# The RWKV recurrence step on ScalarE, and the mixers' steps planned by new durations behind the in-projection matmuls

## The chip, the cores and the metric

One core of a Trainium2 chip runs the whole program. It has five engines that each take their own instructions in order: TensorE (PE, matmuls; its weight loads are PEld), VectorE (DVE), ScalarE (ACT), GpSimd (POOL) and SyncE (SP), which issues the DMA transfers. The metric is the device time of one execution in microseconds (us), lower is better; the median of several runs is compared.

## The reference

One layer on 1024 tokens of width 1024: RMSNorm, a projection of every token to the inputs of three kinds of heads, the three mixers side by side, an output projection, a SwiGLU feed-forward, and a final norm, all in float32.

```python
h = rmsnorm(x, g1);  p = h @ w_in            # P_COLS columns, split in three
y = concat(mlstm_group(p_m), retention_group(p_r), rwkv7_group(p_w))
x = x + y @ w_out
x = x + swiglu(rmsnorm(x, g2));  out = rmsnorm(x, g3)
# RWKV-7, per frame t and head, state S (64 x 64):
S = S * w_t - (S kk_t) (kk_t * a_t)^T + v_t k_t^T;   y_t = S r_t
```

The RWKV recurrence is the one long serial dependence: six heads (three pairs), 1024 frames. The kernel takes it in chunks of 64 frames: inside a chunk a unit triangular 64 x 64 matrix is inverted, and from chunk to chunk a state of 64 x 64 per head is carried.

## The kernel before

**Phases.** The span has three parts. Until some 746 us the in-projection runs and the mixers run between its matmuls; then a rest of the output projection until some 811 us; then the feed-forward until the end. Only the first part is touched by the change. Every float32 product of a projection is made of three matmuls with operands split in a high and a low part: `split_hi` on ACT (L90, `whi`), `split_lo` on DVE (L93, `wlo`), matmuls L119 to L121 (512 columns) and L729 to L731 (256 columns), which all write a tile named `acc`. These are called dense matmuls here.

**What sets the order.** `weave` (L131) is a planner that runs in Python when the program is built. Each stream is a generator; a stream gives up its turn with `yield cost, latency`: its cost advances a planned clock, and it is due again after the latency. Streams `rwkv_chain`, `rwkv_inverse`, `rwkv_prep`, `rwkv_out`, `norms` and `attention` have precedence in this order; the in-projection's streams (`sharing`) fill what is left. `signal` and a yielded name let one stream wait for another. The instructions come out in the order in which the planner reached them, a scheduler then sets each engine's own order from that, and each engine keeps to it: an instruction whose wait isn't over holds up what stands behind it. The planner's numbers are `PART`, `LAT`, `CHAIN`, `INV`, `ATT`, `NORM`, `MIX` and the literals in the yields.

**The RWKV streams.** Per pair of heads and half of the sequence `rwkv_prep` makes, for 8 chunks, the matrices E (by DVE from the gram matmuls L460; transposes L480) and X. `rwkv_inverse` fetches the triangular blocks back from DRAM as MN, with one DMA (L507, 512 KB, each value on several partitions), has ACT copy a part of it to R (four copies, L509), and then solves on DVE in a row of dependent steps (L514 to L522); the result goes to DRAM (r_d) and comes back into E by four DMAs (L532); two transposes on DVE (L535) and matmuls L540 end it. `rwkv_chain` does the 48 steps of the recurrence (3 pairs x 16 chunks), each of five pieces of TensorE with a hand-over between: L581 (state against kappa), ACT copies the result to `pm` (L583); L586 with pm gives u, ACT copies u into X (L592, L593); L597 and L600 give the state's increment and the output; DVE makes the next state from old state, decay and increment and writes it straight into the next step's X (L607, two halves), POOL copies it to `st` (L609, two halves), and ACT copies the output to `yw` (L610) and squares it (L611). The next step's L581 reads that X.

**The other mixers.** `attention` runs the mLSTM and the retention by chunks of 128 tokens: `mlstm_load` fetches q, k, v and the gate weights `w`; it adds the causal mask (POOL L860) and takes exponentials (ACT L863), and `mlstm_chunk` uses them. `mlstm_gates` sends a few numbers by DMA through DRAM and scans them on DVE (L798). `rot` is the rotary table, one load of 512 KB at the start.

## Time and profile before

| | us |
|---|---|
| median of 3 runs (range) | 1515.08 (1514.54 to 1521.72) |
| the profiled execution | 1521.67 |
| its span, first to last instruction | 1519.9 |
| PE busy in it | 1425.6 (94%) |
| DVE, ACT, POOL busy | 892.4 (59%), 556.2 (37%), 437.9 (29%) |

The profiled execution is one of the runs; the trace's numbers add up to its span, 1519.9 us, with 1.8 us around it. Busy shares are means over three phases with different limits, so the reader has to look at the stretch that the change touches, at what the idle time of TensorE there ended with, and at the clock that was granted to TensorE: it has two levels, 2.4 GHz (shown as 1.0) and 1.2 GHz (shown as 0.5).

### The profile page before, as it was taken

The numbers are of one execution on the slowest core, as the hardware profiler recorded it, in microseconds if no ns is written. First come the engines' busy times: TensorE is split into PE (matmuls) and PEld (weight loads), VectorE is DVE, ScalarE is ACT, GpSimd is POOL, SyncE is SP. The second block draws the span as 40 slices with busy tenths as digits, with TensorE's granted clock in tenths as the row PEclk, the third lists the DMA queues.
The fourth block names the chain that finished last, engine by engine and source line by source line (L and its number), as shares of the span: only waits on it lengthen the run. The fifth ranks groups of instructions, "written<-read, shape, count | busy, mean of one in ns | idle before, by whom it ended". The sixth has DMA issues, their size and how long they took to land.

```text
span 1519.9 us, 23085 instructions
## 1 busy us (share of the span) xinstructions
PE 1425.6 (94%) x8434; PEld 1161.3 (76%) x8434; DVE 892.4 (59%) x1762; ACT 556.2 (37%) x1202; POOL 437.9 (29%) x539
## 2 busy tenths in 40 slices
PE   7998799789998998999998999999999998999996
PEld 5777577777777887887777887888888886887886
DVE  6457567458847756645468555555555565347434
ACT  6353334333432133244456333333333344224222
POOL 3211013234424333333545433344444420000000
PEclk9999999999978889899999999999999999999998
DMA  5142122334422244354632222222222247337333
GB/s 209 43 136 66 50 80 74 83 89 112 122 59 68 85 129 124 106 161 142 220 112 85 96 83 83 72 73 78 83 84 83 83 168 255 93 95 238 98 97 111
DMA packets 122269, 164.55 MB, mean 108 GB/s; under 512 B 38028, under 2 KB 70956, under 8 KB 120876
## 3 DMA queue, kind: packets, MB, share of 16 engines
q1 hardware_dynamic: 122156, 163.08, 33.5%
q8 instruction: 66, 1.08, 0.3%
q14 instruction: 47, 0.39, 0.1%
HBM read 124.75 MB, written 38.29 MB: 107 GB/s over the span
## 4 chain that ended last, share of the span: by engine, by line
PE 53%; DVE 3%; POOL 2%; DMA 2%; issue 1%; ACT 0%; POOLq 0%; DVEq 0%; SPq 0%; ACTq 0%
PE acc L1171 5%; PE acc L1172 5%; PE acc L1173 5%; PE chain L1365 5%; PE chain L1364 5%; PE chain L1366 5%; PE misc L1172 4%; PE misc L1171 4%; PE misc L1173 4%; PE acc L119 2%; PE acc L121 2%; PE acc L120 2%; DVE act L93 1%; PE acc L729 1%; PE acc L731 1%
## 5 line engine op out<-in xcount | busy, mean ns | idle before, releaser
L93 DVE TENSOR_TENSOR wlo<-wraw,whi 128x512 fp32r<-128x512 f32 (+1 forms) x210 | 147.9, 707 | 138.3 <-ACT whi L90 137.1
L90 ACT ACTIVATE whi<-wraw 128x512 fp32r<-128x512 f32 (+1 forms) x210 | 128.1, 612 | 226.3 <-PE chain L1365 117.9
L729 PE MATMUL acc<-whi,act 128*128 128x256 f32 (+1 forms) x512 | 161.3, 318 | 4.4 <-ACT whi L90 3.4
L90 ACT ACTIVATE whi<-rg 128x512 fp32r<-128x512 f32 x128 | 79.8, 631 | 228.7 <-POOL rg L1232 90.0
L730 PE MATMUL acc<-wlo,act 128*128 128x256 f32 (+1 forms) x512 | 155.4, 305 | 5.2 <-DVE wlo L93 5.2
L119 PE MATMUL acc<-act,whi 128*128 128x512 f32 x352 | 152.3, 433 | 7.0 <-ACT whi L90 6.2
L93 DVE TENSOR_TENSOR wlo<-rg,whi 128x512 fp32r<-128x512 f32 x128 | 93.1, 728 | 108.1 <-ACT whi L90 105.9
L731 PE MATMUL acc<-whi,act 128*128 128x256 f32 (+1 forms) x512 | 153.0, 300 | 0.0
L1364 PE MATMUL chain<-act,whi 128*128 128x512 f32 (+1 forms) x374 | 144.3, 386 | 4.0 <-ACT act L90 4.0
L120 PE MATMUL acc<-act,whi 128*128 128x512 f32 x352 | 145.5, 413 | 1.5 <-DVE act L252 1.5
L121 PE MATMUL acc<-act,wlo 128*128 128x512 f32 x352 | 145.7, 414 | 1.1 <-DVE wlo L93 1.1
L1365 PE MATMUL chain<-act,whi 128*128 128x512 f32 (+1 forms) x374 | 144.0, 385 | 0.5 <-DVE act L93 0.5
L1366 PE MATMUL chain<-act,wlo 128*128 128x512 f32 (+1 forms) x374 | 143.8, 384 | 0.0
L1171 PE MATMUL acc<-act,whi 128*128 128x512 f32 x352 | 139.3, 396 | 3.4 <-ACT pre L1432 2.7
L1173 PE MATMUL acc<-act,wlo 128*128 128x512 f32 x352 | 138.8, 394 | 0.0
L1172 PE MATMUL acc<-act,whi 128*128 128x512 f32 x352 | 138.5, 394 | 0.0
L729 PEld LDWEIGHTS acc<-whi,act 128*128 128x128 f32 x512 | 104.3, 205 | 12.1 <-ACT whi L90 3.9
L730 PEld LDWEIGHTS acc<-wlo,act 128*128 128x128 f32 x512 | 105.0, 206 | 9.2 <-DVE wlo L93 6.7
L731 PEld LDWEIGHTS acc<-whi,act 128*128 128x128 f32 x512 | 105.2, 206 | 1.0
L1172 PE MATMUL misc<-act,whi 128*128 128x512 f32 x264 | 104.1, 394 | 0.0
L1171 PE MATMUL misc<-act,whi 128*128 128x512 f32 x264 | 104.0, 394 | 0.0
L1173 PE MATMUL misc<-act,wlo 128*128 128x512 f32 x264 | 103.8, 393 | 0.0
(327 smaller groups left out, 2835.9 us busy)
## 6 DMA issues: line engine op xcount, KB each, us to landing
wraw<-in_w_down SPq DMA_DIRECT2D x85, 256.0 KB, 2.7
rg<-in_w_gate SPq DMA_DIRECT2D x22, 512.0 KB, 4.9
rg<-in_w_up SPq DMA_DIRECT2D x22, 512.0 KB, 5.0
a_dram<-work SPq DMA_DIRECT2D x41, 256.0 KB, 2.2
wraw<-in_w_tm SPq DMA_DIRECT2D x40, 256.0 KB, 3.0
rg<-a_dram SPq DMA_DIRECT2D x10, 1024.0 KB, 6.1
v_dram<-vt SPq DMA_DIRECT2D x64, 128.0 KB, 1.9
wraw<-in_w_out SPq DMA_DIRECT2D x32, 256.0 KB, 3.2
```

Source lines behind the costliest of these rows:

```text
L90: S.activation(hi, src, AF.Copy, scale=scale)
L93: (eng or V).tensor_tensor(lo, src, hi.bitcast(F32), ALU.subtract)
L119: PE.matmul(ps, lhsT=hi, rhs=xh[:, k, :], start=(k == 0), stop=False)
L729: PE.matmul(o, lhsT=xh[h][:, k, sl], rhs=w[k][0], start=(k == 0), stop=False)
L730: PE.matmul(o, lhsT=xh[h][:, k, sl], rhs=w[k][1], start=False, stop=False)
L731: PE.matmul(o, lhsT=xl[h][:, k, sl], rhs=w[k][0], start=False, stop=(k == KT - 1))
L1171: PE.matmul(ps, lhsT=hi, rhs=hi_x[:, k, :], start=(start and k == 0), stop=False, skip_group_check=True)
L1172: PE.matmul(ps, lhsT=hi, rhs=lo_x[:, k, :], start=False, stop=False, skip_group_check=True)
L1173: PE.matmul(ps, lhsT=lo, rhs=hi_x[:, k, :], start=False, stop=(stop and k == 3), skip_group_check=True)
L1364: PE.matmul(ps, lhsT=hi, rhs=hi_a[:, sl], start=(f == 0), stop=False)
L1365: PE.matmul(ps, lhsT=hi, rhs=lo_a[:, sl], start=False, stop=False)
L1366: PE.matmul(ps, lhsT=lo, rhs=hi_a[:, sl], start=False, stop=(f == FT - 1))
```

## The change

1. **Order.** Each step of a stream that is not the in-projection's is now issued inside `tc.issue_after(dense[0])`: its matmuls stay behind the last in-projection matmul that the planner had reached. `late(engine)` does the same against the last instruction of one engine, for the inverse's first DVE step, its transposes, the mask of the mLSTM weights, one product in `rwkv_out` and one split in `norms`. Nearly all costs and latencies of the planner are new.
2. **The chain.** E's layout is changed so that increment and output come from one pair of matmuls with 128 columns of weights (L627). ACT copies the increment alone into the next step's X (L633, two halves). What the decayed old state adds is made by POOL (`sd`, one product) and two more matmuls into the next step's tile (L619). DVE makes the next `st` beside that (L636, two halves), from the same PSUM tile; the POOL copies are gone. The output copy and its square are now two halves each (L640, L641). TensorE has 10 matmuls in a step before and after.
3. **The inverse.** R comes by a DMA of its own, 128 KB in pieces of 128 B, instead of the four ACT copies.
4. **The rest.** The mLSTM weights' mask and exponentials are made after the chunk before (`mlstm_weights`) instead of with the loads. `rot` comes in 24 loads of 64 KB, one per token tile and group, instead of one load. The gram matmuls keep their order.

```diff
-    clock, events = [0.0], {}
+            dense[0] = PE.matmul(ps, lhsT=lo, rhs=xh[:, k, :], start=False, stop=(k == KT - 1)).ins
+
+
+
+
+
+    clock, events = [10.0], {}
...
+            with nullcontext() if s[2] in sharing or dense[0] is None else tc.issue_after(dense[0]):
+                got = next(s[2], None)
             if s is holder:
...
-    PART = 6 * 0.214
+    PART, TOK = 6 * 0.23, 12 * 0.47e-3
...
     NT = 9
-    LAT = 0.93
-    CHAIN, INV, ATT, NORM, MIX = 3.51, 20.16, 3.09, 3.26, 1.28
...
-        yield 0.9, 5.5
+            V.tensor_tensor(E[rows, :, kap(q)], c3(kk)[rows], er[rows, :, 0:64], ALU.mult)
+            G.tensor_tensor(E[rows, :, rcp(q)], c3(r)[rows], er[rows, :, 1:65], ALU.mult)
+        yield 1.2, 7.0
...
+            prev = None
+                    with tc.issue_after(prev.ins) if prev else nullcontext():
+                        prev = PE.matmul(g4[:, c, :], lhsT=kb[rows, c0 + c, :, :].rearrange("p a t -> p (a t)"),
+                                         rhs=E[rows, c0 + c, 256 + 128 * q:384 + 128 * q], start=True, stop=True)
...
                 SY.dma_start(out=MN, in_=ab_d.rearrange("b q c s t -> (b q c) (s t)").unsqueeze(0).broadcast_to([4, 32, 1024]))
-                for g in range(4):
-                    S.copy(out=R[lane(g)], in_=MN[lane(g), g::4, :])
-                yield 0.0, 8.0
+                SY.dma_start(out=R, in_=ab_d.rearrange("b q c (j g) t -> g (b q c) j t", g=4))
+                yield 0.0, 11.0
 
                 mf = MN.rearrange("p s t -> p (s t)")
                 tv = ev.tile([P, 516], F32, name="rt", tag="ev")[:, 0:480].rearrange("p (s t) -> p s t", t=32)
-                V.tensor_tensor(tv, mf[:, 34:34 + 15 * 66:66].unsqueeze(2).broadcast_to([P, 15, 32]), MN[:, 2:31:2], ALU.mult)
+                with late(V):
+                    V.tensor_tensor(tv, mf[:, 34:34 + 15 * 66:66].unsqueeze(2).broadcast_to([P, 15, 32]), MN[:, 2:31:2], ALU.mult)
                 V.tensor_tensor(MN[:, 1:30:2], MN[:, 1:30:2], tv, ALU.add)
                 for u in range(1, 31, 2):
...
-                yield 0.0, 7.5
+                        SY.dma_start(out=E[blk(q, b), :, col(q, b)], in_=r_d[b, q].rearrange("c s t -> s c t"))
+                yield 0.0, 9.0
                 for q in range(2):
-                    V.transpose(out=T11[blk(q, 0)], in_=E[blk(q, 0), :, q, col(0)])
+                    with late(V):
...
-                chn = chain_tile()
+
+
+                chn = chain_tile() if first else nxt
+                both = lambda q: slice(128 + 64 * q, 192 + 64 * q)
                 pm = sb.tile([P, 64], F32, name="pm", tag="pm", bufs=2)
                 for q in range(2):
-                    PE.matmul(chn[rows_of(1 - q), 0:64], lhsT=E[:, c, q, 128:192], rhs=X[:, c, q, :],
-                              start=True, stop=True, skip_group_check=True)
+                    PE.matmul(chn[rows_of(1 - q), 0:64], lhsT=E[:, c, kap(q)], rhs=X[:, c, q, :],
+                              start=first, stop=True, skip_group_check=True)
                 S.copy(out=pm, in_=chn[:, 0:64])
-                yield 0.2, LAT
+                if not last:
+                    nX, nE, n = (X, E, c + 1) if c < 7 else (hv[i, 1]["X"], hv[i, 1]["E"], 0)
+                    sd = sb.tile([P, 64], F32, name="sd", tag="sd", bufs=2)
+                    G.tensor_scalar(sd, st, dl[:, c:c + 1], None, ALU.mult)
+                yield 0.4, LAT[0]
                 for q in range(2):
-                    PE.matmul(chn[rows_of(q), 64:128], lhsT=E[rows_of(1 - q), c, q, 192:256], rhs=pm[rows_of(1 - q), :],
+                    PE.matmul(chn[rows_of(q), 64:128], lhsT=E[rows_of(1 - q), c, rcp(q)], rhs=pm[rows_of(1 - q), :],
                               start=False, stop=True, skip_group_check=True)
+                S.copy(out=X[0:64, c, 0, :], in_=chn[0:64, 64:128])
+                S.copy(out=X[64:128, c, 1, :], in_=chn[64:128, 64:128])
+                yield 0.2, LAT[1]
                 for q in range(2):
                     d, o = rows_of(q), rows_of(1 - q)
-                    PE.matmul(chn[o, 192:256], lhsT=E[d, c, q, 192:256], rhs=st[d, :], start=False, stop=False,
+                    PE.matmul(chn[o, both(q)], lhsT=E[d, c, rcp(q)], rhs=st[d, :], start=False, stop=False,
                               skip_group_check=True)
-                S.copy(out=X[0:64, c, 0, :], in_=chn[0:64, 64:128])
-                S.copy(out=X[64:128, c, 1, :], in_=chn[64:128, 64:128])
-                yield 0.2, LAT
-                for q in range(2):
-                    if not last:
-                        PE.matmul(chn[rows_of(q), 128:192], lhsT=E[:, c, q, 0:64], rhs=X[:, c, q, :], start=False, stop=True,
+                if not last:
+                    nxt = chain_tile()
+                    for q in range(2):
+                        d, o = rows_of(q), rows_of(1 - q)
+                        PE.matmul(nxt[o, 0:64], lhsT=nE[d, n, kap(q)], rhs=sd[d, :], start=True, stop=False,
                                   skip_group_check=True)
                 for q in range(2):
-                    PE.matmul(chn[rows_of(1 - q), 192:256], lhsT=E[:, c, q, 64:128], rhs=X[:, c, q, :], start=False, stop=True,
-                              skip_group_check=True)
+                    o = rows_of(1 - q)
+                    if last:
+                        PE.matmul(chn[o, both(q)], lhsT=E[:, c, 64 + 64 * q:128 + 64 * q], rhs=X[:, c, q, :], start=False,
+                                  stop=True, skip_group_check=True)
+                    else:
+                        PE.matmul(chn[:, both(q)], lhsT=E[:, c, 128 * q:128 * q + 128], rhs=X[:, c, q, :], start=False,
+                                  stop=True, skip_group_check=True)
                 if not last:
-                    nX, n = (X, c + 1) if c < 7 else (hv[i, 1]["X"], 0)
                     nst = sb.tile([P, 64], F32, name="st", tag="st", bufs=2)
                     for q in range(2):
                         d = rows_of(q)
-                        V.scalar_tensor_tensor(nX[d, n, q, :], in0=st[d, :], scalar=dl[d, c:c + 1],
-                                               in1=chn[d, 128:192], op0=ALU.mult, op1=ALU.add)
-                        G.tensor_copy(nst[d, :], nX[d, n, q, :])
-                S.copy(out=yw[:, c % 4, :], in_=chn[:, 192:256])
-                S.activation(sb.tile([P, 64], F32, name="ysq", tag="ysq"), chn[:, 192:256], AF.Square,
-                             accum_out=var[:, c % 4:c % 4 + 1])
+                        S.copy(out=nX[d, n, q, :], in_=chn[d, both(q)])
+                    for q in range(2):
+                        d = rows_of(q)
+                        V.scalar_tensor_tensor(nst[d, :], in0=st[d, :], scalar=dl[d, c:c + 1], in1=chn[d, both(q)],
+                                               op0=ALU.mult, op1=ALU.add)
+                for q in range(2):
+                    o = rows_of(1 - q)
+                    S.copy(out=yw[o, c % 4, :], in_=chn[o, both(q)])
+                    S.activation(sb.tile([P, 64], F32, name="ysq", tag="ysq")[o, :], chn[o, both(q)], AF.Square,
+                                 accum_out=var[o, c % 4:c % 4 + 1])
                 if not last:
                     st = nst
                 if c % 4 == 3:
                     norm_factor(yw, var, 4, 64e-5)
                     signal(f"yw{len(yws)}", 8.0)
                     yws.append(yw)
-                yield 0.4, CHAIN
+                yield 0.6, CHAIN
             signal(f"chain{i}{h}", 1.0)
 
     yws = []
...
-                    G.tensor_tensor(add, add, ga, ALU.mult)
...
+                    with late(G):
+                        G.tensor_tensor(add, add, ga, ALU.mult)
...
             h, sl = chunk_of(t)
+            if g in (2, 3, 4):
+                rot = at.tile([P, P], F32, name="rot", tag="rot", bufs=2)
...
-
-    rot = at.tile([P, KT, P], F32, name="rot", tag="rot")
-    SY.dma_start(out=rot, in_=a["rot"])
...
+            ws.append(w)
+        return qT, kT, MV, ws
+
+    def mlstm_weights(c, ws):
+        for q, w in enumerate(ws):
             G.tensor_tensor(w, w, cc("causal").unsqueeze(1).broadcast_to([P, 2, P]), ALU.add)
             for p in range(2):
                 hd = 2 * p + q
                 S.activation(w[:, p, :], w[:, p, :], AF.Exp, scale=-1.0, bias=mg["gs"][:, c, hd:hd + 1])
-            ws.append(w)
-        return qT, kT, MV, ws
...
-                split_hi(yh[:, 5 + i], yw)
+                yield 0.0, 3.0
+                with late(S):
+                    split_hi(yh[:, 5 + i], yw)
...
-        mlstm = ("mlstm", 2.6, mlstm_load, mlstm_chunk, mlstm_finish, None)
-        ret = ("ret", 4.0, ret_load, ret_chunk, ret_finish, ret_store)
+        def weigh(t, args):
+            if len(args) == 4:
+                with late(G):
+                    mlstm_weights(t, args[-1])
+
+        mlstm = ("mlstm", 4.2, mlstm_load, mlstm_chunk, mlstm_finish, None)
+        ret = ("ret", 5.0, ret_load, ret_chunk, ret_finish, ret_store)
         for (name, cost, load, chunk, finish, store), start, ts in (
             (mlstm, "qkv_m", range(KT)), (ret, "qkv_r0", range(4)), (ret, "qkv_r1", range(4, KT)),
         ):
             yield start
             args, before = load(ts.start), None
             yield 0.0, 6.0
+            weigh(ts.start, args)
+            yield 0.0, 2.0
             for t in ts:
                 y = chunk(t, *args)
                 if t < ts.stop - 1:
                     args = load(t + 1)
                 yield cost, ATT
+                if t < ts.stop - 1:
+                    weigh(t + 1, args)
                 if store and before:
                     yield f"proj{t // 4}"
                     store(t - 1, *before)
```

Where it moves instructions. First ACT, a step of the third pair's chain, before, with the last inverse's copies of R in it:

```order
L610 COPY yw<-chain 128x64 [waits DVE_49,PE_49]
L611 ACTIVATE ysq,yvar<-chain 128x64 [waits Activation_49]
L755 ACTIVATE vt<-acc,rhalf 128x256 [waits DMAHW5_49,PE_49]
L482 COPY E<-misc 128x8x64 [waits PE_49] x2
L755 ACTIVATE vt<-acc,rhalf 128x256 [waits DMAHW6_49,PE_49]
L583 COPY pm<-chain 128x64 [waits PE_49]
L509 COPY R<-MN 32x256 [waits DMAHW6_49]
L509 COPY R<-MN 32x256 x3
L755 ACTIVATE vt<-acc,rhalf 128x256 [waits PE_49]
L592 COPY X<-chain 64x64 [waits PE_49]
L593 COPY X<-chain 64x64 [waits Pool_49]
```

And ACT after, a step of the same pair's chain:

```order
L633 COPY X<-chain 64x64 [waits PE_49]
L633 COPY X<-chain 64x64
L978 COPY rT<-misc 128x384 [waits PE_49]
L978 COPY rT<-misc 128x384 [waits DMAHW4_49,PE_49]
L640 COPY yw<-chain 64x64 [waits DVE_49]
L641 ACTIVATE ysq,yvar<-chain 64x64 [waits Activation_49]
L640 COPY yw<-chain 64x64
L641 ACTIVATE ysq,yvar<-chain 64x64 [waits Activation_49]
L599 COPY pm<-chain 128x64 [waits PE_49]
L90 ACTIVATE whi<-wraw 128x512 [waits DMAHW1_49,PE_49]
L90 ACTIVATE whi<-wraw 128x512 [waits DMAHW2_49,PE_49]
L608 COPY X<-chain 64x64 [waits PE_49]
```

The R copies are gone from the row; the X copy for the next step (L633) stands first and waits for TensorE alone, but the two yw copies still wait for DVE, and the next step's pm copy (L599) stands behind them.

Next DVE near the end of the first inverse (tq are its transposes, MN and rt belong to the next inverse), before:

```order
L93 TENSOR_TENSOR wlo<-wraw,whi 128x512 [waits DMAHW4_49,PE_49,Activation_49]
L317 TENSOR_TENSOR rp<-acc,RS 128x512 [waits PE_49,Pool_49]
L514 TENSOR_TENSOR rt<-MN 128x480 [waits DMAHW7_49,DMAHW5_49,DMAHW0_49]
L93 TENSOR_TENSOR wlo<-wraw,whi 128x512 [waits DMAHW6_49,Activation_49]
L535 STREAM_TRANSPOSE tq<-E 32x256 [waits DMAHW7_49]
L336 SCALAR_TENSOR_TENSOR t<-rp,vec,t 128x512 [waits Activation_49,Pool_49]
L515 TENSOR_TENSOR MN<-MN,rt 128x15x32 [waits DVE_49,Activation_49]
L535 STREAM_TRANSPOSE tq<-E 32x256 [waits DMAHW1_49]
```

And after:

```order
L548 STREAM_TRANSPOSE tq<-E 32x256 [waits DMAHW0_49]
L548 STREAM_TRANSPOSE tq<-E 32x256 [waits DMAHW2_49]
L93 TENSOR_TENSOR wlo<-wraw,whi 128x512 [waits PE_49,Activation_49]
L323 TENSOR_TENSOR rp<-acc,RS 128x512 [waits PE_49]
L93 TENSOR_TENSOR wlo<-wraw,whi 128x512 [waits DMAHW7_49,Activation_49]
L342 SCALAR_TENSOR_TENSOR t<-rp,vec,t 128x512 [waits Activation_49,Pool_49]
L636 SCALAR_TENSOR_TENSOR st<-st,dl,chain 64x64 [waits PE_49,Activation_49]
L636 SCALAR_TENSOR_TENSOR st<-st,dl,chain 64x64
L323 TENSOR_TENSOR rp<-acc,RS 128x512 [waits PE_49]
L342 SCALAR_TENSOR_TENSOR t<-rp,vec,t 128x512 [waits Activation_49,Pool_49]
L93 TENSOR_TENSOR wlo<-wraw,whi 128x512 [waits DMAHW5_49,PE_49,Activation_49]
L636 SCALAR_TENSOR_TENSOR st<-st,dl,chain 64x64 [waits PE_49,Activation_49]
```

The transposes now stand ahead of the next inverse's first step (L514 before, L526 after, two rows further on than is shown), and two pairs of state updates of the chain (L636) stand between them.

## Rows read from the trace of the kernel before

**Rows 1.** Windows: us, busy us (instructions) of five engines, granted clock, DMA share, GB/s.

```profile
0.00:746.00 746.00, 677.55 (x5155) 554.28 (x5156) 471.25 (x1173) 281.65 (x746) 229.48 (x395) 0.92 0.34 104
...
811.00:1520.00 709.00, 686.85 (x3021) 557.27 (x3019) 377.19 (x535) 239.70 (x398) 175.42 (x123) 0.99 0.33 108
```

**Rows 2.** TensorE's waits, 0 to 720 us: total us, times, longest.

```profile
PE misc L540 <- DVE tq L535: 10.5, 3, 7.7
PE chain L597 <- ACT X L593: 7.8, 3, 6.0
PE chain L586 <- ACT pm L583: 7.6, 5, 2.0
...
PE misc L460 <- DVE E L468: 5.2, 3, 4.3
PE acc L730 <- DVE wlo L93: 5.2, 7, 1.7
PE chain L581 <- DVE X L607: 4.4, 1, 4.4
PE acc L729 <- ACT whi L90: 3.4, 2, 3.0
```

**Rows 3.** The same waits within 290 to 310 us, where an inverse begins.

```profile
PE acc L730 <- DVE wlo L93: 2.5, 2, 1.7
PE chain L586 <- ACT pm L583: 2.0, 1, 2.0
PE chain L597 <- ACT X L593: 1.5, 1, 1.5
```

**Rows 4.** Timeline of ACT: start, duration, engine, line, operation, [idle before, releaser].

```profile
372.17 0.69 ACT L863 ACTIVATE w<-w,gtok 128x128 f32<-128x128 f32 x2 [6.02 <-POOL w L860]
...
594.03 1.65 ACT L509 COPY R<-MN 32x256 f32<-32x256 f32 x4 [6.80 <-DMA MN<-ab_d]
...
596.30 0.21 ACT L593 COPY X<-chain 64x64 f32<-64x64 f32 x1
```

**Rows 5.** Timeline of TensorE, dense matmuls ahead of that stop and behind it.

```profile
590.14 0.28 PE L730 MATMUL acc<-wlo,act 128*128 128x256 f32 x1
590.26 0.28 PE L731 MATMUL acc<-whi,act 128*128 128x256 f32 x1
...
598.21 0.41 PE L730 MATMUL acc<-wlo,act 128*128 128x256 f32 x1
598.42 0.41 PE L731 MATMUL acc<-whi,act 128*128 128x256 f32 x1
```

**Rows 6.** Windows of TensorE alone: us, busy us (instructions), granted clock, DMA share, GB/s.

```profile
307.00:314.00 7.00, 6.40 (x31) 0.51 0.54 165
...
419.60:429.90 10.30, 10.30 (x42) 0.50 0.51 124
...
491.30:501.60 10.30, 10.12 (x54) 0.50 0.37 121
...
593.70:600.60 6.90, 4.04 (x24) 0.51 0.19 61
```

**Rows 7.** Timeline of DVE at the end of the first inverse and in the gates.

```profile
161.24 0.66 DVE L514 TENSOR_TENSOR rt<-MN 128x480 f32<-128x480 f32 x1 [7.81 <-DMA E<-r_d]
...
162.54 0.44 DVE L535 STREAM_TRANSPOSE tq<-E 32x256 f32<-32x256 f32 x1
...
279.65 0.16 DVE L798 TENSOR_TENSOR_SCAN mp<-m 4x8 f32<-4x8 f32 x1 [5.50 <-DMA m<-bl_d]
```

**Rows 8.** Groups by line, 0 to 746 us: busy us, mean ns, idle before, what ended it.

```profile
L607 DVE SCALAR_TENSOR_TENSOR X<-st,dl,chain 64x64 f32<-64x64 f32 x90 | 25.0, 277 | 13.5 <-PE chain L600 9.3 <-ACT whi L90 2.6
...
L611 ACT ACTIVATE ysq<-chain 128x64 f32<-128x64 f32 x48 | 11.1, 231 | 0.0
...
L583 ACT COPY pm<-chain 128x64 f32<-128x64 f32 x48 | 10.1, 210 | 49.6 <-PE chain L581 49.5
L593 ACT COPY X<-chain 64x64 f32<-64x64 f32 x48 | 9.9, 207 | 1.0
L611 ACT ACTIVATION_READ_ACCUMULATOR ysq<-chain 128x1 f32 x48 | 9.8, 205 | 0.0
```

**Rows 9.** ACT's waits over the whole span: total us, times, longest.

```profile
ACT yw L610 <- DVE X L607: 62.8, 24, 10.1
```

**Rows 10.** DMA issues: tile, queue, count, KB each, median us from issue to landing.

```profile
E<-r_d SPq DMA_DIRECT2D x24, 32.0 KB, 1.9
```

62 lines of the change are left out of this document (32 added, 30 removed).

## The prediction, made before the changed kernel was run

> **What bounds the kernel now.** I read the windows first: TensorE is busy in 678 of the 746 us in which the mixers run between in-projection matmuls, and its granted clock there is 0.92 on the mean; in the feed-forward it is 0.99, and nothing of the change reaches that phase [rows 1]. ACT is busy in 282 of the 746 us, so no engine but TensorE is a bound by its sum. Two things can be won in these 746 us: the 68 us in which TensorE stands (746 - 678), and the half clock. A mean of 0.92 between levels 1.0 and 0.5 is (1 - 0.92) / 0.5 x 746 = 119 us at the low level. What a low microsecond costs is read from two pairs of starts: a 256-column matmul follows the one before after 0.12 us at the high clock and after 0.21 us at the low one [rows 5], so a little over 0.4 of each low microsecond is lost, some 48 us in all. Next I read who ended TensorE's waits [rows 2], and for each of them what stood ahead of the late instruction on its engine.
>
> **The inverse's start: R no longer goes through ACT.** At 594.03 ACT begins four copies of R after it had waited 6.80 us for the DMA of MN, and the chain's X copy stands behind them and is done at 596.5 [rows 4]; TensorE waits 6.0 us for that X [rows 2]. The same stands at 290 to 310 us (2.0 + 1.5, and 2.5 for weights that DVE splits late) [rows 3], and a wait of 3.0 us for `whi` is behind the same copies near 490 us [rows 2]. Sum: 6.0 + 3.5 + 2.5 + 3.0 = **15 us**. After the change no instruction of ACT waits for MN. DVE still does (L526), and with it the chain's next state update. But in the order of DVE one more step of the chain stands between the prep's end and L526 than before in each of the last four inverses, so MN has that much longer to land. I keep 10 as the low end, where a third of it comes back through DVE, and take 15.
>
> **The weights of the mLSTM.** At 372.17 ACT had waited 6.02 us for POOL's mask on w, which itself waited for a DMA, with the chain's pm copy behind [rows 4]. L586 waits for pm five times, 7.6 us in all [rows 2]; one of these, 2.0 us, belongs to R [rows 3]. The other four are **5.6 us**. Mask and exponentials are now placed after the chunk, against the last instruction of POOL, and the order of ACT has them behind a chain step. Low end 3, where ACT finds w late again once or twice; I take 5.6.
>
> **The first inverse's end, and the first gram matmuls.** L540 waited 7.7 us for a transpose on DVE [rows 2] that stood behind a wait of 7.81 us [rows 7]. In the new order TensorE has 48 instead of 32 of the 512-column matmuls between the prep's transposes and the inverse's first matmul: 16 more at twice 0.12 us, so **3.8 us** of more cover. The transposes now stand ahead of the next inverse's first step. But their data come by the same queue of SP behind the MN load, so I don't count more; ends 0 and 7.7. For the wait of 4.3 us on L468 [rows 2], five more matmuls lie ahead: 5 x 0.24 = **1.2 us**, ends 0 and 4.3.
>
> **The clock.** Three low stretches begin in or right behind waits that go: 307 to 314, 491.3 to 501.6 and 593.7 to 600.6 us [rows 6], in all 24 us, with 0.4 lost of each: 10 us. But from 419.6 to 429.9 us the clock is 0.50 while TensorE is busy throughout, with 42 records in 10.3 us [rows 6]: a wait is not what keeps it low there, and the small matmuls of the mixers remain. I take half, **5 us**; low end 0. The Trainium skill's page "TensorE: Matmul & The Clock Gate", section "HAM oscillation — how this bites in real kernels", ties the low clock to waits of TensorE for data. By that rule all of the 48 us would follow the waits and the sum would be 1488.5 - 43 = 1445 us; the row at 419.6 speaks against it.
>
> **The chain's step.** It adds work to ACT: two X copies of 0.21, and yw, square and its read in two halves instead of one, 0.21 + 0.23 + 0.21 [rows 8]. That is 1.06 us in each of 47 steps, 50 us, on an engine that is idle in 464 of the 746: hidden by its sum. TensorE keeps its 10 matmuls, and POOL loses its copies, on which TensorE did not wait. The new X depends on ACT alone: 0.41 us instead of two steps of DVE of 0.28. But what counts is the cover, and that was cut. From state matmul to the next u matmul the order has typically 18 dense matmuls, before 24: 18 x 0.24 = 4.3 us. In that time come two X copies (0.41), DVE's two updates (0.55), which read the same PSUM tile, two yw copies and squares (1.3), which wait for DVE, and pm (0.21): 2.5 us, with five hand-overs some 3.1 (an estimate). About 1.2 us is left for any of these engines to be late, where 24 matmuls left some 3. In eight of the 47 steps no dense matmul stands between the state matmul and the next step's first one, only 6 to 12 small ones; there the two X copies and a hand-over show by some 0.5 us each, **4 us lost**. Ends: 0, and 18 (half of the first rival below).
>
> **Small edits.** The scan of the gates waits 5.50 us for a DMA on DVE [rows 7], and one wait of 4.4 us of L581 stands behind it [rows 2]. The new order has the scan just as well ahead of the state update; nothing is counted. The `rot` load in 24 parts, the split ahead of `norms` and the product moved in `rwkv_out` lie on queues for which TensorE hardly waits: nothing, and under 2 us if not. The end of the chain is not a bound: the last dense matmul of this phase comes behind it in both orders.
>
> **Sum.** 15 + 5.6 + 3.8 + 1.2 + 5 - 4 = 26.6 us. The profiled execution took 1521.7 us and would take 1495.1; it lies 6.6 above the median of 1515.1, and from that the forecast is 1515.1 - 26.6 = **1488.5 us**.
>
> **The rivals.**
> *DVE stays in the chain, and slower.* ACT's yw copy waited for DVE's X 24 times, 62.8 us, up to 10.1 [rows 9]: DVE is 2.6 us late in each of these on the mean. Before, that had 3 us of cover, and TensorE seldom paid. Now yw stands ahead of pm in 38 of 48 steps and the cover leaves 1.2: 24 x (2.6 - 1.2) = 34 us of new waits. If every third of them is followed by 7 low microseconds, 8 x 7 x 0.4 = 22 more. The gains without the 4 already taken off are 30.6: 1515 - 31 + 34 + 22 = 1540; without the clock 1518. It decides from DVE being late by over some 2.3 us in half the steps. Against it: in many of these steps the mixers' own matmuls lengthened the cover, and the gates and the R copies made the longest. For it: DVE is the busier of the two. Chance 0.14.
> *The waits only move.* A PE that no longer waits for X takes its weights sooner, and they come through the same ACT, now with 50 us more, and DVE: `whi` and `wlo` already ended 8.6 us of waits [rows 2]. If they take back four fifths of the gain: 1510. For it: L90 and L93 stand in row with the chain's copies. Against it: ACT idles in three fifths of this phase. Chance 0.10.
> *The small pieces of R.* A quarter as many pieces of the same 128 B, 32 KB, land in 1.9 us [rows 10]; four times that, 7.6, would be behind MN, while DVE has 1.3 us of its own work there, so at worst DVE waits 6.3 us in each inverse, of which 1.2 is covered: 6 x 5.1 = 31 us, and 1515 - 27 + 31 = 1519. The Trainium skill's "DMA: Bandwidth & Descriptors", section "Why small descriptors are slow (HBM only)", speaks for this, since each small piece pays a fixed cost; no run so far shows R's own load. Against it: the four transfers of [rows 10] run beside each other and land in 1.9 us. Chance 0.04.
> *The clock comes back with the waits.* If the low level falls away wherever the mixers' matmuls now alternate with dense ones, two thirds of the 48 us come back instead of 5: 1488.5 - 27 = 1461. Against it the row at 419.6 [rows 6]. Chance 0.10.
>
> **How the numbers follow.** The forecast has 0.62. Its low end has every upper end (L540 7.7, L468 4.3, no loss in the chain) and the clock's two thirds: 1515 - 15 - 5.6 - 7.7 - 4.3 - 32 = 1450. The high end has every lower end and the chain's 18: 1515 - 10 - 3 + 18 = 1520. That holds the second rival and the fourth, and leaves out the upper part of the first: 1450 to 1520. About 0.5%, 7.6 us, is what a measurement of this kernel can tell from no change. Faster than 1507.5: 0.62 + 0.10 = 0.72. Within: the moved waits and R's pieces, 0.14. Slower: the first rival, 0.14.
>
> **What the profile after would show.** Right: no wait of L597 behind R, no wait on POOL's w with pm behind; waits of L606 for pm under 10 us in all; the mean clock up to 746 us between 0.92 and 0.95. Wrong: L606 waiting for pm, with ACT's yw waiting for DVE's st, in many steps by 1 to 3 us (first rival); L729 and L119 waiting for `whi` by over 20 us (second); L531 waiting for R's DMA (third); a clock of 0.97 (fourth).

## The result, and the profile of the changed kernel

The changed kernel takes 1525.46 us (median of 20 runs, 1515.98 to 1537.84), the one before 1519.21 us in as many runs beside it (1511.34 to 1524.86). The ratio is **1.005, 95% interval 1.003 to 1.0069**: a little slower, by some 6 to 8 us, where 26.6 us less were forecast. It is outside the range that was given.

The profiled execution of the changed kernel, 1515.98 us, is the fastest of its 20 runs. It was therefore profiled once more, as e12, in a run of 1527.7 us that is nearer to the median. Both show the same waits; they differ in the clock. TensorE's clock over the whole span is 0.968 in the first and 0.957 in e12, and its median over the 20 runs is 0.961.

First the windows of the mixers' part, of the first profile and then of e12; the columns are those of [rows 1].

```profile
0.00:746.00 746.00, 681.73 (x5183) 555.68 (x5184) 471.59 (x1179) 321.84 (x962) 226.10 (x353) 0.95 0.36 110
```

```profile
0.00:746.00 746.00, 681.41 (x5100) 555.46 (x5101) 465.09 (x1165) 316.58 (x952) 220.50 (x346) 0.93 0.34 105
```

ACT has 35 to 40 us more than before: 50 were worked out, and the copies of R, 24 of 0.40 us, went. The clock went from 0.92 to 0.95 and 0.93. But TensorE stands nearly as long as before: 746 - 681.6 = 64 us, against 68. Counted over the same work, from its first matmul to the end of the out-projection, its idle time is 66.0 us before, 63.5 in the first profile and 63.8 in e12. Here is who ended its waits within 0 to 720 us, first profile, to be laid beside [rows 2]:

```profile
PE acc L763 <- ACT whi L90: 13.3, 5, 6.8
PE acc L119 <- ACT whi L90: 6.1, 1, 6.1
PE misc L471 <- DVE E L479: 5.8, 2, 5.3
PE chain L606 <- ACT pm L599: 5.2, 2, 3.7
PE misc L910 <- DMA mq<-mqk_dram: 4.7, 1, 4.7
PE misc L414 <- DVE t L412: 3.6, 1, 3.6
...
PE misc L553 <- DVE tq L548: 2.3, 1, 2.3
...
PE chain L597 <- ACT X L633: 0.2, 1, 0.2
```

and of e12:

```profile
PE acc L763 <- ACT whi L90: 12.7, 5, 6.6
...
PE chain L606 <- ACT pm L599: 5.8, 2, 4.2
```

The kernel before has this line too, which is not among those of [rows 2]:

```profile
PE acc L119 <- ACT whi L90: 6.2, 1, 6.2
```

The waits behind R's copies and behind the exponentials are gone, that of the first inverse's end fell from 7.7 to 2.3. In their place the waits for `whi` doubled (19.4 us in all, before 6.2 + 3.4 = 9.6), one for mq came, and those for t grew from 1.8 to 3.6; for pm 5.2 of 7.6 us are left, at other places. So the sum of waits is nearly what it was, with other names on it. Where the larger ones come from is seen on the queues. SP's timeline after an inverse's issue, near 294 us, and near 382 us (start, duration of the issue, line, transfer):

```profile
294.20 0.54 SPq L519 DMA_DIRECT2D MN<-ab_d  x1
294.78 0.51 SPq L520 DMA_DIRECT2D R<-ab_d  x1
295.39 8.80 SPq L685 DMA_DIRECT2D yw_dram<-gate  x1
...
305.26 0.38 SPq L101 DMA_DIRECT2D wraw<-in_w_tm  x1
...
381.61 0.57 SPq L519 DMA_DIRECT2D MN<-ab_d  x1
382.24 0.56 SPq L520 DMA_DIRECT2D R<-ab_d  x1
382.86 8.32 SPq L101 DMA_DIRECT2D wraw<-in_w_tm  x1
391.22 0.95 SPq L883 DMA_DIRECT2D mq<-mqk_dram  x2
```

The issue behind R's takes 8 to 9 us, where others take 0.4. The packets show what it stands for: R's first piece starts 6.7 to 7.4 us after R's issue in five of the six inverses, when the last pieces of MN start, and R's pieces then go out within 3.0 to 3.7 us; in the same five SP's next issue ends 1.0 to 1.3 us before the last of them starts. What is late behind it: DVE waits for MN and then for R (first row of each pair below), ACT for a weight that was issued at 305.26, and TensorE for that weight and for mq, issued at 391.22.

```profile
303.38 0.66 DVE L526 TENSOR_TENSOR rt<-MN 128x480 f32<-128x480 f32 x1 [2.14 <-DMA MN<-ab_d]
...
306.42 0.22 DVE L531 TENSOR_TENSOR rt<-R,MN 128x60 f32<-128x60 f32 x1 [1.69 <-DMA R<-ab_d]
...
390.34 0.66 DVE L526 TENSOR_TENSOR rt<-MN 128x480 f32<-128x480 f32 x1 [5.51 <-DMA MN<-ab_d]
```

```profile
308.57 0.63 ACT L90 ACTIVATE whi<-wraw 128x512 fp32r<-128x512 f32 x1 [6.19 <-DMA wraw<-in_w_tm]
```

```profile
309.25 0.58 PE L763 MATMUL acc<-whi,act 128*128 128x256 f32 x1 [6.81 <-ACT whi L90]
...
395.06 1.23 PE L910 MATMUL misc<-mq 64*128 64x128 f32 x8 [4.66 <-DMA mq<-mqk_dram]
```

MN itself takes as long as ever: from its issue at 294.20 to the DVE step that reads it, 303.38, are 9.2 us, and from 381.61 to 390.34 8.7 us. In the kernel before it was 9.6 (issued at 584.40, read at 594.03, [rows 4]). Two more waits hang on it. The 3.6 us for t stand behind a wait of 3.66 us of DVE for MN at 117 us. The 3.7 us for pm near 509 us stand behind `yw` on ACT and the state update on DVE, and DVE had stood 5.91 us for a `gate` that was issued between MN and R.

The second thing is the chain's own time on TensorE. Its five matmul groups, busy us and mean ns, in the kernel before:

```profile
L581 PE MATMUL chain<-X,E 128*64 128x64 f32 x192 | 17.8, 255 | 4.4 <-DVE X L607 4.4
L586 PE MATMUL chain<-pm,E 64*64 64x64 f32 x192 | 16.9, 247 | 7.7 <-ACT pm L583 7.6
L597 PE MATMUL chain<-X,E 128*64 128x64 f32 x180 | 16.0, 260 | 7.8 <-ACT X L593 7.8
L600 PE MATMUL chain<-X,E 128*64 128x64 f32 x192 | 15.6, 238 | 0.0
L590 PE MATMUL chain<-st,E 64*64 64x64 f32 x192 | 15.0, 224 | 0.5 <-POOL st L609 0.5
```

and in the changed kernel:

```profile
L627 PE MATMUL chain<-X,E 128*128 128x64 f32 x180 | 30.3, 290 | 0.0
...
L606 PE MATMUL chain<-pm,E 64*64 64x64 f32 x192 | 17.2, 247 | 5.6 <-ACT pm L599 5.2 <-ACT E L562 0.2
L597 PE MATMUL chain<-X,E 128*64 128x64 f32 x192 | 16.9, 250 | 0.2 <-ACT X L633 0.2
L613 PE MATMUL chain<-st,E 64*64 64x64 f32 x192 | 16.0, 244 | 0.0
L619 PE MATMUL chain<-sd,E 64*64 64x64 f32 x180 | 13.3, 223 | 0.4 <-POOL sd L603 0.4
```

With the last steps' 1.0 us the second list sums to 94.7, the first to 81.3. As matmuls overlap, the time that they keep TensorE is better counted from each one's start to the next one's start, without idle time. These are called slots here: **69.4 us against 54.5**, 15 us more, with less of it at the low clock (3.1 us against 8.3). By group, the new `sd` pair has 10.1 us of it; L606 and L613 together have 22.7 where L586 and L590 had 20.0; L627 with the last steps' matmuls has 23.4 where L597 and L600 had 20.2; the first group is 1.0 us shorter.

### The profile page after: what moved, and what is told of

The parts are those of the page before. It is cut to its first block, busy times and chain, and to the rows that moved or that the text cites. A ratio compares the mean times of both kernels' runs of the same rounds, so it can differ in the third digit from the quotient of the medians.

```text
span 1514.2 us, 23293 instructions
## 1 busy us (share of the span) xinstructions
PE 1423.1 (94%) x8434; PEld 1157.6 (76%) x8434; DVE 888.3 (59%) x1762; ACT 593.5 (39%) x1412; POOL 431.3 (28%) x494
## 4 chain that ended last, share of the span: by engine, by line
PE 66%; DMA 9%; DVE 8%; issue 5%; POOL 4%; ACT 2%; SPq 0%; POOLq 0%; DVEq 0%; ACTq 0%
PE acc L1216 5%; PE acc L1217 5%; PE acc L1218 5%; PE chain L1410 5%; PE chain L1409 5%; PE chain L1411 5%; PE misc L1217 4%; PE misc L1216 4%; PE misc L1218 4%; PE acc L119 4%; PE acc L121 3%; PE acc L120 3%; PE acc L763 2%; DMA MN<-ab_d 2%; PE acc L764 2%
## 5 line engine op out<-in xcount | busy, mean ns | idle before, releaser
L93 DVE TENSOR_TENSOR wlo<-wraw,whi 128x512 fp32r<-128x512 f32 (+1 forms) x210 | 144.6, 692 | 144.0 <-ACT whi L90 143.4
L763 PE MATMUL acc<-whi,act 128*128 128x256 f32 (+1 forms) x512 | 155.8, 307 | 13.3 <-ACT whi L90 13.3
L119 PE MATMUL acc<-act,whi 128*128 128x512 f32 x352 | 151.5, 431 | 6.8 <-ACT whi L90 6.1
L764 PE MATMUL acc<-wlo,act 128*128 128x256 f32 (+1 forms) x512 | 151.7, 297 | 1.0 <-DVE wlo L93 0.9
L765 PE MATMUL acc<-whi,act 128*128 128x256 f32 (+1 forms) x512 | 148.9, 292 | 0.0
L763 PEld LDWEIGHTS acc<-whi,act 128*128 128x128 f32 x512 | 100.7, 198 | 19.8 <-ACT whi L90 14.9
L764 PEld LDWEIGHTS acc<-wlo,act 128*128 128x128 f32 x512 | 101.1, 198 | 5.9 <-issue 2.7
L765 PEld LDWEIGHTS acc<-whi,act 128*128 128x128 f32 x512 | 101.2, 198 | 0.8
```

The source lines that it names most:

```text
L93: (eng or V).tensor_tensor(lo, src, hi.bitcast(F32), ALU.subtract)
L119: PE.matmul(ps, lhsT=hi, rhs=xh[:, k, :], start=(k == 0), stop=False)
L763: PE.matmul(o, lhsT=xh[h][:, k, sl], rhs=w[k][0], start=(k == 0), stop=False)
L764: PE.matmul(o, lhsT=xh[h][:, k, sl], rhs=w[k][1], start=False, stop=False)
L765: dense[0] = PE.matmul(o, lhsT=xl[h][:, k, sl], rhs=w[k][0], start=False, stop=(k == KT - 1)).ins
```

## The experiments

Ratios are to the kernel before, which ran beside each; intervals are 95%.

**Theories.** *Queue*: the DMA of R, 1024 pieces of 128 B, holds up SP behind the slow MN load, and the loads behind are late. *MN*: MN's own 9 us are what everything near an inverse waits for in the end; which engine or queue is named only depends on what stands behind the wait. *Chain on TensorE*: the new step costs 15 us of a TensorE that is the bound. *The prediction's view*: R's copies on ACT cost 15 us. *DVE in the chain* (the prediction's first rival): `yw` waits for DVE, and pm stands behind.

### e1: R copied by ACT again, in the changed kernel

```diff
-                SY.dma_start(out=R, in_=ab_d.rearrange("b q c (j g) t -> g (b q c) j t", g=4))
+                for g in range(4):
+                    S.copy(out=R[lane(g)], in_=MN[lane(g), g::4, :])
```

> The changed kernel with the old way to R: four copies on ACT out of MN instead of a DMA of its own. Queue theory (R's 1024 pieces of 128 B stand behind the slow MN load and hold up SP's next issue for 8 to 9 us, in four of six inverses; the loads behind come late, which costs TensorE the 6.8 + 4.7 + 3.7 = 15 us of waits for whi, mq and pm): no issue of SP over 4 us behind MN, these three waits gone, and 5 to 15 us faster than the changed kernel, ratio to before 0.995 to 1.002, if the copies do not bring their own waits back. The prediction's view (the copies cost 15 us on ACT): 10 to 15 us slower than the changed kernel, ratio 1.012 to 1.015.

Measured: 1527.9 us, ratio 1.0081 (1.004 to 1.0122), beside 1.005 of the changed kernel: no difference that can be told. The long issues of SP behind MN went, but for one of 8.2 us in the second inverse, and the mq wait with them. Instead:

```profile
PE acc L764 <- ACT whi L90: 12.6, 5, 5.5
PE chain L607 <- ACT pm L600: 12.4, 3, 6.4
...
PE misc L554 <- DVE tq L549: 5.4, 1, 5.4
...
PE chain L598 <- ACT X L634: 3.4, 1, 3.4
```

pm went from 5.2 to 12.4. The queue theory (a gain) does not hold, and the prediction's view (a ratio of 1.012 to 1.015) lies at the very end of the interval: by the middles it makes 2 to 5 us of difference who waits for MN, ACT or SP.

### e4: R by a DMA, the only edit to the kernel before

```diff
-                for g in range(4):
-                    S.copy(out=R[lane(g)], in_=MN[lane(g), g::4, :])
+                SY.dma_start(out=R, in_=ab_d.rearrange("b q c (j g) t -> g (b q c) j t", g=4))
```

> The kernel before with one edit: R by a DMA of its own instead of the four ACT copies. The prediction's view: the 15 us of waits behind the copies go, ratio 0.990 (0.988 to 0.994). Queue theory: these waits go, but SP is held up by 8 us behind MN and R, and waits for weights and loads come in their place: ratio 0.997 to 1.003.

Measured: 1524.6 us, ratio 1.0036 (1.001 to 1.0061). The prediction's largest term alone, worth 15 us there, gives nothing, even a little loss. TensorE's waits, 0 to 720 us, in the profiled run, which was the fastest of the twelve (1514.9 us):

```profile
PE chain L596 <- ACT X L592: 10.3, 2, 10.1
...
PE chain L580 <- DVE X L606: 9.3, 2, 4.9
```

The 4.9 us at 590.9 stand where the 6.0 of [rows 2] stood: ACT is free, but DVE stands for MN with the chain's X behind,

```profile
586.16 0.66 DVE L513 TENSOR_TENSOR rt<-MN 128x480 f32<-128x480 f32 x1 [5.19 <-DMA MN<-ab_d]
...
590.56 0.27 DVE L606 SCALAR_TENSOR_TENSOR X<-st,dl,chain 64x64 f32<-64x64 f32 x1
```

and the 10.1 at 305 is ACT standing for the mLSTM's w, whose DMA was issued late behind MN and R (an issue of SP at 285.1 took 7.8 us):

```profile
301.99 0.40 ACT L862 ACTIVATE w<-w,gtok 128x128 f32<-128x128 f32 x1 [10.38 <-POOL w L859]
```

### e2: MN by four DMAs, in the changed kernel

```diff
-                SY.dma_start(out=MN, in_=ab_d.rearrange("b q c s t -> (b q c) (s t)").unsqueeze(0).broadcast_to([4, 32, 1024]))
+                for g in range(4):
+                    SY.dma_start(out=MN[lane(g)], in_=ab_d.rearrange("b q c s t -> (b q c) s t"))
```

> The changed kernel with MN loaded by four DMAs of 128 KB (32 partitions each) instead of one of 512 KB whose source is repeated four times. In the traces so far MN's 128 pieces of 4 KB start at some 20 in a microsecond, though each takes 0.19 us. Queue theory: if the one repeated source is what makes MN slow, it lands in 4 us or less instead of 9, SP is not held up, and the time falls by 10 to 20 us against the changed kernel: ratio to before 0.992 to 0.998. If the pieces come as slowly as before, MN lands after 9 us again and nothing changes: ratio 1.003 to 1.007.

Measured: 1484.7 us, ratio **0.9767** (0.9732 to 0.9802), some 43 us below the changed kernel (1.005 - 0.9767 = 2.8%; 41 by the medians), twice what was expected. Each of the four DMAs now lands in

```profile
DMA to landing us min/median/max: 3.1/3.6/4.3
```

after its own issue, and DVE waits for none of them. TensorE's waits:

```profile
PE misc L471 <- DVE E L479: 8.1, 3, 5.8
PE acc L119 <- ACT whi L90: 6.2, 1, 6.2
PE acc L764 <- ACT whi L90: 5.3, 4, 2.8
```

The wait of L763 (here L764) for `whi` fell from 13.3 to 5.3; mq, t, pm and tq no longer stand in the list with more than 1 us; the idle time of TensorE up to the end of the out-projection fell from 63.5 to 37.9 us. That is 26 of the 43 us. The rest is of the size of the clock: the low level has 61 us up to there, 78 in the first profile of the changed kernel and 119 in e12, and at 0.4 of each low microsecond the 58 us less than in e12 are 23. The packets show why MN is quicker. Its 128 pieces of 4 KB take some 0.2 us each. In the one DMA of the changed kernel four of them are under way together for most of the time, and at most 25 to 28 start within a microsecond. In the four DMAs up to 15 to 18 are under way together, and 54 to 72 start in the busiest microsecond (five inverses; in the sixth the four were not issued together). SP's next issue behind R takes 2.6 to 3.2 us in four inverses, where it took 8 to 9.

### e11: MN by two DMAs, each with its source repeated twice

```diff
-                SY.dma_start(out=MN, in_=ab_d.rearrange("b q c s t -> (b q c) (s t)").unsqueeze(0).broadcast_to([4, 32, 1024]))
+                for g in range(2):
+                    SY.dma_start(out=MN[64 * g:64 * g + 64], in_=ab_d.rearrange("b q c s t -> (b q c) (s t)").unsqueeze(0).broadcast_to([2, 32, 1024]))
```

> The changed kernel with MN by two DMAs of 256 KB, each with its source repeated twice. In one DMA (repeat 4) pieces of 4 KB start at 20 in a microsecond, in four DMAs (no repeat) at 60 to 80. If each DMA has its own limit of 20: two give 40, MN lands in 5 to 6 us. If the repeat sets on how many engines a DMA is spread: two DMAs with a repeat of 2 give together 20 again, MN lands after 8 to 9 us.

Measured, in one run: 1563.7 us. The last piece of MN starts 13.7 to 15.8 us after the issue in all six inverses, where it is 8.0 to 8.6 us with one DMA of repeat 4 and 3.7 to 4.7 in five of the six with four DMAs (in the sixth they were not issued together). Both expectations named were too kind, and the second is nearer: the repeat, as the outermost dimension, goes with the number of pieces that are under way together. It is four for 69 to 82% of the time with one DMA of repeat 4, and two for 81 to 92% of it with the two DMAs of repeat 2, both together. 128 pieces x 0.19 us / 2 = 12 us, and over four 6 us, agree with what the trace shows for the last piece less the first (11.3 to 14.4, and 6.3 to 7.2). So more DMAs are not what helps; no repeat is. SP's next issue behind R now takes 13.2 to 15.7 us in four inverses: it follows MN. The Trainium skill has the rule. "DMA: Bandwidth & Descriptors", section "Why a DMA increments its semaphore by 16 and not by 1", says that the number of DMA engines is the largest one up to 16 that divides the outermost dimension of both sides, and that they are the lowest-numbered ones. Its section "Rules for kernel authors" warns of a leading repeat of c, which holds the whole DMA on at most c engines. The runs agree in the number of pieces under way; they do not show which engines those are.

### e5: MN by four DMAs, the only edit to the kernel before

```diff
-                SY.dma_start(out=MN, in_=ab_d.rearrange("b q c s t -> (b q c) (s t)").unsqueeze(0).broadcast_to([4, 32, 1024]))
+                for g in range(4):
+                    SY.dma_start(out=MN[lane(g)], in_=ab_d.rearrange("b q c s t -> (b q c) s t"))
```

> The kernel before with one edit: MN by four DMAs of 128 KB instead of one of 512 KB with its source repeated. MN theory (the wait that ends last around each inverse is MN's landing, 9 us, and not ACT's copies, which merely stood behind it): with MN landing in under 4 us the waits at L597, L586 and part of L540 shrink although the copies are still there, and the time falls by 12 to 25 us, ratio 0.984 to 0.992. If the copies themselves were the cost (four of 0.40 us and their place on ACT): under 7 us, ratio over 0.995.

Measured: 1492.2 us, ratio **0.9822** (0.9798 to 0.9846), 27 us less, a little more than expected. R's copies are still on ACT, and the wait of L597 (here L598) for X is under 1 us. TensorE's waits:

```profile
PE chain L587 <- ACT pm L584: 5.3, 1, 5.3
...
PE chain L582 <- DVE X L608: 3.9, 1, 3.9
...
PE chain L598 <- ACT X L594: 0.8, 2, 0.6
```

The 5.3 us for pm, near 365 us, stand behind the exponentials of the mLSTM's w, for which ACT had waited 9.38 us.

### e7: MN by four DMAs and R by ACT, in the changed kernel

```diff
-                SY.dma_start(out=MN, in_=ab_d.rearrange("b q c s t -> (b q c) (s t)").unsqueeze(0).broadcast_to([4, 32, 1024]))
-                SY.dma_start(out=R, in_=ab_d.rearrange("b q c (j g) t -> g (b q c) j t", g=4))
+                for g in range(4):
+                    SY.dma_start(out=MN[lane(g)], in_=ab_d.rearrange("b q c s t -> (b q c) s t"))
+                for g in range(4):
+                    S.copy(out=R[lane(g)], in_=MN[lane(g), g::4, :])
```

> The changed kernel with MN by four DMAs and R copied by ACT again. MN theory: once MN lands in under 4 us the copies wait for little and R's own load is worth next to nothing: within 5 us of e2, ratio to before 0.974 to 0.981. The prediction's view (the copies on ACT cost 15 us): 10 to 15 us slower than e2, ratio 0.984 to 0.987.

Measured: 1489.8 us, ratio 0.9793 (0.9766 to 0.9819). Beside e2, 0.9767, R's own DMA is worth 4 us by the middles, and the intervals overlap. That is within the 5 us of the MN theory; the 10 to 15 us of the prediction's view are not seen.

### e3: the old chain step, in the changed kernel

The step's body is that of the kernel before, with E's new layout, and the step's planner numbers are those of before (0.93 and 3.51):

```diff
-                        PE.matmul(nxt[o, 0:64], lhsT=nE[d, n, kap(q)], rhs=sd[d, :], start=True, stop=False,
...
-                        PE.matmul(chn[:, both(q)], lhsT=E[:, c, 128 * q:128 * q + 128], rhs=X[:, c, q, :], start=False,
+                        PE.matmul(chn[rows_of(q), 128:192], lhsT=E[:, c, 192 * q:192 * q + 64], rhs=X[:, c, q, :], start=False, stop=True,
...
-                        S.copy(out=nX[d, n, q, :], in_=chn[d, both(q)])
+                        V.scalar_tensor_tensor(nX[d, n, q, :], in0=st[d, :], scalar=dl[d, c:c + 1],
```

> The changed kernel with the chain's step as it was before: DVE writes the next X, POOL copies st, four narrow matmul pairs where the new step has sd and the 128-column pair; its own planner numbers too (0.93, 3.51). TensorE theory (the new step's matmuls take 69.5 us of TensorE instead of 54.5, at no more than the same number): the sum of the chain's slots returns to 53 to 57 us and the time falls by 10 to 17 us against the changed kernel, ratio to before 0.993 to 0.999. If the chain is hidden as the prediction says: no change, ratio 1.003 to 1.007. If DVE in the chain was the worse way: slower, ratio over 1.008.

Measured: 1510.9 us, ratio **0.9942** (0.9917 to 0.9967): 1.1 points, some 16 us, below the changed kernel. The chain's slots sum to 54.4 us, 15.0 less. Three of its groups:

```profile
L601 PE MATMUL chain<-pm,E 64*64 64x64 f32 x192 | 18.1, 256 | 1.7 <-ACT pm L598 1.7
L596 PE MATMUL chain<-X,E 128*64 128x64 f32 x192 | 17.6, 252 | 3.8 <-DVE X L622 3.8
L612 PE MATMUL chain<-X,E 128*64 128x64 f32 x180 | 16.4, 256 | 2.2 <-ACT X L608 2.2
...
```

The waits for DVE's X are 3.8 us in all, so DVE in the chain costs far less than the matmuls that free the chain from it. TensorE's idle time is as long as in the changed kernel (64.6 us), so it is the slots that the time follows here; the planner numbers of the step went back with its body, and no run parts the two.

### e9: the wide pair split in two narrow ones, with MN by four DMAs

```diff
-                        PE.matmul(chn[:, both(q)], lhsT=E[:, c, 128 * q:128 * q + 128], rhs=X[:, c, q, :], start=False,
+                        PE.matmul(chn[rows_of(q), both(q)], lhsT=E[:, c, 192 * q:192 * q + 64], rhs=X[:, c, q, :], start=False,
...
+                        PE.matmul(chn[rows_of(1 - q), both(q)], lhsT=E[:, c, 64 + 64 * q:128 + 64 * q], rhs=X[:, c, q, :],
```

> As e2 (the changed kernel, MN by four DMAs), but the pair of matmuls with 128 columns of weights is split into two pairs with 64, as the old step had them; sd and its two matmuls stay. In e2's trace the chain's slots sum to 70.3 us, in the old step's kernels to 54.4. If the wide pair is what costs: the sum falls to 64 to 66 and the time by 3 to 6 us, ratio to before 0.973 to 0.975. If sd's two extra matmuls (10.1 us of slots) are the cost: the sum stays at 68 to 73 and the time within 3 us of e2.

Measured: 1485.5 us, ratio 0.979 (0.9764 to 0.9815), e2 being 0.9767: no gain. The slots fell by 4 us, from 70.3 to 66.1, with as much of them at the low clock (3.3 us against 3.1). But TensorE's idle time up to the end of the out-projection rose from 37.9 to 47.0 us, so the 4 us do not show in the time. The groups:

```profile
L628 PE MATMUL chain<-X,E 128*64 128x64 f32 x180 | 16.2, 247 | 0.0
...
L632 PE MATMUL chain<-X,E 128*64 128x64 f32 x180 | 13.9, 225 | 0.0
L620 PE MATMUL chain<-sd,E 64*64 64x64 f32 x180 | 13.3, 223 | 0.1
```

In busy time the two narrow pairs are as dear as the wide one, 16.2 + 13.9 = 30.1 beside 30.5 in e2. In slots they are cheaper, 18.6 us against 22.8. So the wide pair does both jobs in half the matmuls and saves nothing; it has some 4 of the 15 us, and the larger part, 10.1, is the sd pair's. That either part turns into time by itself is not shown: e3 takes out both.

### e10: the mLSTM weights made late, in the kernel before with MN by four DMAs

```diff
-            G.tensor_tensor(w, w, cc("causal").unsqueeze(1).broadcast_to([P, 2, P]), ALU.add)
...
+    def mlstm_weights(c, ws):
...
+                if t < ts.stop - 1:
+                    weigh(t + 1, args)
```

> As e5 (the kernel before, MN by four DMAs), with mask and exponentials of the mLSTM weights made after the chunk instead of with the loads; nothing else. The prediction's 5.6 us for the waits of L586 behind the exponentials, if it holds without the slow MN: 3 to 7 us faster than e5, ratio to before 0.977 to 0.980. If these waits also came from elsewhere: within 3 us of e5, ratio 0.980 to 0.985.

Measured: 1485.1 us, ratio 0.9773 (0.9735 to 0.9811), beside e5's 0.9822 (0.9798 to 0.9846): 7 us less by the middles, with intervals that touch. The wait of 5.3 us of e5 for pm is gone; 1.8 us for pm are left, and TensorE's idle time fell from 46.8 to 40.8 us. That fits the 5.6 us; it is not shown beyond doubt.

### e6 and e8: MN by four DMAs and the old chain step, with and without the tie

e6 joins e2 and e3. e8 also lets the mixers' steps go from the last in-projection matmul:

```diff
-            with nullcontext() if s[2] in sharing or dense[0] is None else tc.issue_after(dense[0]):
-                got = next(s[2], None)
+            got = next(s[2], None)
```

> The changed kernel with both: MN by four DMAs, and the old chain step. If the two losses are independent (e2 fell by some 41 us against the changed kernel, e3 by 14.5): 1525.5 - 41 - 14.5 = 1470, ratio to before 0.966 to 0.970. If the new chain step is what keeps the chain out of TensorE's way once MN is quick (DVE and the POOL copies late in the old one): no better than e2, ratio 0.975 or more.

> As e6, but the mixers' steps are no longer tied behind the last in-projection matmul (the planner's new numbers stay). If the tie is a part of the gain: 5 to 20 us slower than e6. If only the numbers matter: within 4 us of e6.

Measured: e6 1476.4 us, 0.9717 (0.9687 to 0.9747); e8 1471.6 us, **0.9686** (0.9663 to 0.971). Beside e2 the old step gives 8 us here by the medians, half of what e3 showed, though the chain's slots fell by 18 us, from 70.3 to 52.4. The two profiled runs, 1484.9 and 1467.2 us, are 17.7 us apart at the same clock over the whole span, 0.973, and with nearly the same idle time (37.9 and 36.6 us). The other five runs of e6 had 0.964 to 0.970, those of e2 0.971 to 0.980: so the missing half goes with the clock. Why e6 is granted less of it is not known. The tie is worth nothing that shows; without it the middle is even lower, inside the intervals. e8 is the fastest kernel of the study, 48 us below the one before.

### e12: the changed kernel once more

> The changed kernel once more, for a profile of an ordinary run: the profiled one, 1516.0 us, was the fastest of 20 with a median of 1525.5. MN theory: again 8 to 9 us from MN's issue to DVE's L526 and SP's next issue held up after R's, in four of six inverses; the extra 10 us lie in waits and in the low clock, not in the chain's slots (69 to 71 us).

Measured: 1527.7 us. The chain's slots are 71.5 us, and MN's last piece starts 7.5 to 9.0 us after its issue in all six inverses; SP's issue behind R takes 7.9 to 9.8 us in four of the six, 8.6 of them at 505.78. The low clock has 119 us up to the end of the out-projection, against 78 in the first profile and 126 in the kernel before. At the 0.4 of a microsecond that was read for each low one, the 41 us between the two profiles are 16 us, of the same size as the 11.7 us between the runs: the first profile was one of a run with less of the low clock.

## Why the prediction was wrong

**R on ACT, 15 us: the step that failed.** The trace row said "ACT waited 6.80 us for MN", and the prediction put the price on the four copies and took the wait away with them. The wait was not for the copies but for MN, and DVE waited for it just as well. The prediction saw that ("DVE still does") and gave a third of the term to it; in fact all of it came back, through DVE in e4, through SP's queue in the changed kernel. Its reason, one more chain step ahead of L526, was too little: DVE still stood 2.1 and 5.5 us near 303 and 390, and 11.3 us for MN in three waits, 10.2 before. The right question was why MN takes 9 us for 512 KB when 256 KB of weights are there in some 3, and the answer was worth 27 us in the kernel before (e5) and 43 in the changed one (e2).

**The third rival** had R's pieces in mind, but as a wait of DVE for R, 31 us in all (it was 2.5 us, 1.7 of them at 306.42). R's 1024 pieces themselves went out in 3.0 to 3.7 us; they stood behind MN. What showed was the queue: SP's next issue stood for 8 us, and the price fell on loads that have nothing to do with the inverse. That makes it one more channel for the same wait, since taking R's DMA away again gave nothing (e1, e7). Its 1519 is the rivals' time that lies nearest to what was measured, by luck. **The second rival**, that the waits only move, is what the list of waits looks like: `whi` at 19.4 us is just short of its sign of over 20 (the 8.6 us that it counted before leave out the 6.2 of L119). But its cause was not ACT's load, as e2 with the same ACT work has 11.5, of which 6.2 stood there before the change too.

**The chain, counted as 4 us lost: mis-sized.** "TensorE keeps its 10 matmuls" counted instructions and not their slots. The step costs TensorE 15 us more, and e3 shows some 16 us of time. The stall that was priced at 4 us, the X copies with no dense matmul between, didn't come (L597 waits for 0.2 us in all). **The first rival**, DVE late and pm behind yw, is there once in size: yw waited for DVE 34.3 us in all, up to 6.8, where it was 62.8 before, and pm cost TensorE 5.2. Its 34 us did not come, so a measured result on its side is no proof of it.

**Terms that held at their own places.** The first inverse's end: 7.7 to 2.3, 5.4 us for 3.8. The first gram wait: 4.3 to nothing over 1.2. The mLSTM weights: no pm wait behind them is left, and e10 agrees with 5.6. The gates: the scan still stands, and the wait has moved to L471, 5.3 us. The clock: 0.92 to 0.93 in e12 and 0.95 in the first profile. The low level has 119 us up to 746 us before, 72 in the first profile and 109 in e12, which at 0.4 of each is 19 us gained in the first and 4 in e12; the forecast had 5. Over the whole span the median clock is 0.961 in the 20 runs of the changed kernel and 0.954 in the 25 runs of the one before beside e1 to e4: (0.961 - 0.954) / 0.5 x 1520 = 21 us, and 0.4 of it 8.5 us, as an estimate for an ordinary run.

**The account.** The forecast took 15 + 5.6 + 3.8 + 1.2 = 25.6 us of waits off. TensorE's idle time fell by some 2 us (66.0 to 63.5 and 63.8): single waits went, and others came in their place, most of the large ones behind MN. The chain's slots cost 15 to 17 us more, where 4 were counted. The clock gave back some 8.5, where 5 were counted. That is 15 to 17 - 2 - 8.5 = 4.5 to 6.5 us slower, and 6 to 8 were measured. e3 agrees: the changed kernel without its new step is at 0.9942, 9 us gained, and the new step takes 16.

What stays open: why the clock differs between runs and kernels as it does (e2, e6); and how much of e8's lead over e5 (1.4 points) is the planner's new numbers and how much the other edits; no run parts them.

## What to carry to other kernels

When an instruction stands for a transfer, ask first why the transfer takes that long, and only then who should stand for it: moving the waiting work off one in-order engine hands the wait to the next engine or queue that holds something behind it. A DMA that repeats its source in the outermost dimension is one to split until no repeat is left: in four parts without one MN was quicker (e2, e5), in two parts that still repeat it was slower (e11). And an edit that takes a hand-over out of a chain by adding matmuls must be priced in slots of the engine that is the bound, not in instructions.
